# GpSimd's low parts of weights in four operations of 256 columns, and in the MLPs only behind the first two blocks

## The chip, the cores and the metric

The kernel runs on one core of a Trainium2 chip. The metric is the device time of one execution in microseconds (us).

## The reference, cut to what matters

A trunk of two layers for 256 tokens of width 1024 in f32. Layer 0 mixes tokens by native sparse attention (16 heads of 64), layer 1 by differential attention (8 heads, two softmax maps each). Every mixer is followed by an MLP of width 4096 with a squared ReLU. Each sub-layer has an RMS norm in front, with shift, scale and gate computed from a vector c (adaLN).

```python
for i in range(DEPTH):
    mod = cond @ w_ada[i] + b_ada[i]
    sh1, sc1, g1, sh2, sc2, g2 = jnp.split(mod, 6, axis=-1)
    h = rms_norm(x, ln_mix_g[i]) * (1.0 + sc1[:, None, :]) + sh1[:, None, :]
    ...
    x = x + g1[:, None, :] * y
    h = rms_norm(x, ln_mlp_g[i]) * (1.0 + sc2[:, None, :]) + sh2[:, None, :]
    x = x + g2[:, None, :] * (jnp.square(jax.nn.relu(h @ w_mlp_in[i])) @ w_mlp_out[i])
```

## The kernel before, in words

**Products in three parts.** Every f32 product of the large layers is made of three products of rounded numbers. A matrix w is split into a high part wh (w rounded to the type float32r) and a low part wl = w - wh, an activation h into hh and hl, and `mm3` (lines 79 to 83) adds wh*hh, wl*hh and wh*hl in PSUM: in the profile these are the matmuls of L81, L82 and L83. So each weight costs a load (L158, issued from SP's queue into a buffer wr), a high part (L202, a cast on ScalarE) and a low part (L206, a subtraction on VectorE or on GpSimd). VectorE is DVE in the profile, GpSimd POOL, ScalarE ACT and TensorE PE.

**Units and their order.** The weights are planned in a list of units of kind "w" of 128 x 1024 numbers (512 KB); the order in which they are planned is the order in which they are loaded and split. There are 32 units up to the end of the first mixer, 64 in an MLP (blocks of 512 columns: four units "up" and four units "dn" each), and 32 in the second mixer. Units of kind "a" and "p" between them are weights of the adaLN: "a" is multiplied by c and summed by VectorE (L227 and L232, 128 x 1024 each). `use(u)` (line 241) hands a unit's parts to its matmuls and first carries the list on to `look[0]` units from u, that is four units beyond u in the MLPs, where `look[0]` is 6; `issue` (line 152) keeps the loads ahead by `ahead_dma[0]`. All of wr, wh, wl and other tiles of this size share 32 buffers, so a load waits until one comes free.

**Which engine makes a low part.** `halves[0]` is a list of pairs (engine of the high part, engine of the low part). `do_unit` counts the "w" units and takes the entry that the count, modulo the list's length, points to:

```python
            pos["split"] += 1
            hi, lo = halves[0][pos["split"] % len(halves[0])]
```

In the mixers the list has two entries, the first with GpSimd (lines 1307 and 1328). `sublayer_end` (line 1167) sets it to VectorE alone for the end of a sub-layer and also makes the first four units of the next one. `mlp` (line 1196) sets it to three entries, the first with GpSimd (line 1294), then calls `up_first(2)` for the first two blocks, whose products are made for one half of the tokens and then the other, and then goes through the blocks with `up` and `down`. High and low parts stand under `tc.high_priority(-50)`: the framework plans each engine's order of instructions when the kernel is built, by its own estimate of their times, and these get a lower priority than what stands around them. On an engine, instructions then run in that fixed order.

**What stands around the lows.** `prenorm` (line 1143) makes the rows of a sub-layer's input: L570 on GpSimd (a power), L572 and L574 (scaling), transposes on TensorE (L1151), L1156 and L1159 (shift and scale), then L1163 (hh) and L1164 (hl) on VectorE, which the matmuls L81 to L83 of the MLP wait for. In the mixers VectorE normalises heads: L805, L305 to L311, L811 and L814 (which reads PSUM), the rotary steps L781, L784 and L785, whose result TensorE transposes (L793). In the first mixer it scales softmax rows (L1043, transposed at L1048); in the second it subtracts the two maps (L1365 to L1367, L1369, transposed at L1375), with L1391 on GpSimd and L1402 behind. L77 makes the low part of activations, L1014 the masked scores, and L920 on GpSimd prepares the compressed blocks (16 operations of 120 columns).

Of the kernel before, what the change touches and what calls it, by code (L numbers as in the profile page):

```python
# [19 lines left out]
F32 = mybir.dt.float32  # L20
# [3 lines left out]
ALU = mybir.AluOpType  # L24
# [18 lines left out]
def body(ctx: ExitStack, tc: tile.TileContext, a):  # L43
    nc = tc.nc
    vec, act, pool, pe = nc.vector, nc.scalar, nc.gpsimd, nc.tensor
# [9 lines left out]
    def bank(tag="tr"):  # L55
        return pp.tile([P, 512], F32, name=tag, tag=tag, bufs={"acc": 4, "sc": 2, "tr": 2}[tag])
# [4 lines left out]
    def w4(name, dt=F32):  # L61

        return wp.tile([P, 1024], dt, name=name, tag="w", bufs=32)
# [4 lines left out]
    def z4():  # L68
        return w4("z4", F32R).rearrange("p (i s) -> p i s", i=4)
# [4 lines left out]
    def split(h, l, src):  # L74

        act.copy(h, src)  # L76
        vec.tensor_tensor(l, src, h.bitcast(F32), op=ALU.subtract)  # L77

    def mm3(out, x, w, start, stop):

        pe.matmul(out, x[0], w[0], start=start, stop=False, skip_group_check=True)  # L81
        pe.matmul(out, x[0], w[1], start=False, stop=False, skip_group_check=True)  # L82
        pe.matmul(out, x[1], w[0], start=False, stop=stop, skip_group_check=True)  # L83
# [7 lines left out]
    halves = [[(act.copy, vec)]]  # L91
# [60 lines left out]
    def issue(n):  # L152
        while pos["dma"] < min(len(items), n):
            i = pos["dma"]
            pos["dma"] += 1
            raws[i] = w4("wr")
            for f, src in items[i]:
                nc.sync.dma_start(f(raws[i]), src)  # L158
# [7 lines left out]
    def ada_pe(rs, n, fin, hold, tag="tr"):  # L166
        m = n // P
        ps = bank(tag)
        for k in range(KT):
            c = k % 4  # L170
            w = rs[k * m // KT].rearrange("p (k n) -> p k n", n=n)[:, k % (KT // m)]
            pe.matmul(ps[32 * c : 32 * c + 32, 0:n], condz[:, k], w, start=k < 4, stop=k >= 4,  # L172
                      skip_group_check=True, tile_position=(0, 32 * c))
        acc = tmp()[:, 0:n]
        act.copy(acc, ps[:, 0:n])
        if hold is None:
            fin(acc)
        else:
            hold.append(lambda: fin(acc, ps[:, n:]))
# [3 lines left out]
    def flush(everything=True):  # L183

        for e in pend:
            e[0] -= 1
        while pend and (everything or pend[0][0] <= 0):
            pend.pop(0)[1]()

    def do_unit(u, hold=None):  # L190
        kind, i = units[u][0:2]
        if kind == "w":
            flush(False)
        issue(i + ahead_dma[0])
        r = raws.pop(i)
        if kind == "w":
            n = units[u][2]
            pos["split"] += 1
            hi, lo = halves[0][pos["split"] % len(halves[0])]
            h, l = (w4(x, F32R)[:, 0:n] for x in ("wh", "wl"))  # L200
            with tc.high_priority(-50):
                hi(h, r[:, 0:n])  # L202

            def low():
                with tc.high_priority(-50):
                    lo.tensor_tensor(l, r[:, 0:n], h.bitcast(F32), op=ALU.subtract)  # L206

            if hold is None:
                low()
            else:  # L210
                hold.append(low)
            done[u] = (h, l)
        elif kind == "p":
            n = units[u][3]
            rs = [r] + [raws.pop(i + j) for j in range(1, n // P)]
            if units[u][4]:
                late.append((rs, n, units[u][2]))
            else:
                ada_pe(rs, n, units[u][2], hold)
        else:  # L220
            _, _, st, k, fin, with_pool = units[u]
            with tc.high_priority(-50):
                if k == 0:
                    st["acc"] = w4("acc")
                c = cond[:, k : k + 1]
                if k == 0:
                    vec.tensor_scalar(st["acc"], r, c, None, op0=ALU.mult)  # L227
                elif with_pool:
                    vec.tensor_scalar(r, r, c, None, op0=ALU.mult)
                    pool.tensor_tensor(st["acc"], st["acc"], r, op=ALU.add)  # L230
                else:
                    vec.scalar_tensor_tensor(st["acc"], r, c, st["acc"], op0=ALU.mult, op1=ALU.add)  # L232
            if k == KT - 1:
                fin(st["acc"])
# [6 lines left out]
    def use(u, only=False):  # L241

        ahead = look[0] if only else 0
        for v in range(u, len(units)):
            if units[v][0] == "w":
                ahead += 1
                if v > u and ahead > look[0] - 1:
                    break
            done_to(v)
            if only:  # L250
                break
        h, l = done.pop(u)
        return lambda c, w: (h[:, c : c + w], l[:, c : c + w])
# [386 lines left out]
    for c0, src in ((0, a["nsa_q_gain"][:, 0:16]), (16, a["nsa_k_gain"][0, 1:2, 0:16]), (32, a["nsa_k_gain"][0, 2:3, 0:16]),  # L640
                    (48, a["diff_q_gain"][:, 0:16]), (64, a["diff_k_gain"][:, 0:16]), (80, a["nsa_b_gate"])):
        n = src.shape[1]
# [553 lines left out]
    def mlp(l):  # L1196
# [4 lines left out]
        def relu2(bk):  # L1201
            r = tmp()
            act.activation(r, bk, AF.Relu)  # L1203
            s2 = tmp()
            act.activation(s2, r, AF.Square)
            return s2

        def up_first(nb):

            zs = [(z4(), z4()) for _ in range(nb)]  # L1210
            hid.update(enumerate(zs))
            ws = {}

            def products(b, t):
                ts = slice(t * P, (t + 1) * P)
                if t == 0:
                    ws[b] = [[use(u) for u in U["up", l, b, f2]] for f2 in range(2)]
                bk = bank("sc")
                for f2 in range(2):
                    for k in range(KT):  # L1220
                        mm3(bk[:, f2 * 256 : f2 * 256 + 256], (hh[:, k, ts], hl[:, k, ts]),
                            ws[b][f2][k // 4](k % 4 * 256, 256), k == 0 and f2 == 0, k == KT - 1)
                return relu2(bk)

            def back(b, t, s2):
                ts = slice(t * P, (t + 1) * P)
                tb = bank()
                for j in range(4):
                    pe.transpose(tb[:, j * P : (j + 1) * P], s2[:, j * P : (j + 1) * P], ident)
                split(zs[b][0][:, :, ts], zs[b][1][:, :, ts], tb.rearrange("p (j s) -> p j s", j=4))  # L1230

            prev = None
            for t in range(2):
                for b in range(nb):
                    s2 = products(b, t)
                    if prev is not None:
                        back(*prev)
                    prev = (b, t, s2)
            back(*prev)
# [51 lines left out]
                    yield t, 2  # L1291

        look[0], ahead_dma[0] = 6, 14
        halves[0] = [(act.copy, pool), (act.copy, vec), (act.copy, vec)]
        nb = 2
        up_first(nb)
        while held:
            held.pop(0)()
        for b in range(1, NB):
            if b >= nb:  # L1300
# [20 lines left out]
                pairs(1, qT1, left.pop()), drain_last()), first)  # L1321
    sublayer_end(second, bks, (0, 0), 0, 1, U["up", 0, 0, 0] + U["up", 0, 0, 1], held)
    acc, last = mlp(0)
    sublayer_end(last, acc, (0, 1), 1, 0, U["dk", 0], held)

# [119 lines left out]
    weave(chain(after(*last), heads("F2 V3 S7 E7 C6 T6 . F3 V4 C7 T7 . F4 V5 . V6 F5 V7 F6 F7")), first)  # L1445
    sublayer_end(second, bks, (1, 0), 1, 1, U["up", 1, 0, 0] + U["up", 1, 0, 1], held)
    acc, last = mlp(1)
    ov = a["out"].rearrange("o (t p) d -> p (o t) d", p=P)
    flush()
# [55 lines left out]
```

## Time and profile before

| | |
|---|---|
| median of three runs | 722.15 us (720.5 to 722.8) |
| the profiled execution's own time | 721.25 us |
| its span in the profile | 719.1 us |
| matmuls | 4263, busy 682.3 us |
| low parts on VectorE, L206 | 132, busy 188.5 us |
| low parts on GpSimd, L206 | 60, busy 157.5 us |
| high parts, L202 | 192, busy 191.9 us |
| adaLN sums on VectorE, L232 | 49, busy 72.4 us |

All times within an execution are counted from the start of the span. The profile gives for each engine the time in which it was busy; in the lists of instructions the number in brackets at a row's end is how long the engine had been idle before it, and what ended that. Times of matmuls overlap, as they are pipelined.

### The profile page before, as it was taken

The page shows a single profiled execution, that of the slowest core. Times are in us where ns is not written, and L with a number is a line of the kernel's source. Part 1 is how long each engine was busy: PE and PEld are TensorE (multiplying, and loading weights), DVE is VectorE, ACT ScalarE, POOL GpSimd, SP SyncE. Part 2 cuts the span into 40 slices and gives each one's busy share as a digit, 9 for nine tenths or more (in the row PEclk, how much of TensorE's full clock was granted, in tenths as well). Part 3 has the DMA queues.
Part 4 walks back from the last instruction along what each step waited for, and adds up shares of the span by engine and source line. Part 5 has one row for each costly group of instructions (what it writes and reads, how often), then busy time and mean ns, then how long its engine had stood idle before and what let it go on. Part 6 is the DMA issues. An engine that isn't in the chain of part 4 may idle for free.

```text
span 719.1 us, 11663 instructions
## 1 busy us (share of the span) xinstructions
PE 682.3 (95%) x4263; PEld 565.1 (79%) x4263; DVE 493.1 (69%) x911; ACT 400.5 (56%) x779; POOL 200.5 (28%) x138
## 2 busy tenths in 40 slices
PE   8999889999988999999999999899979999999997
PEld 7787654656687988999896777667769888998896
DVE  4457879777869598858885987776782874235753
ACT  6646438769565345634453765786566355543650
POOL 4105311002023243233231634223222143323430
PEclk9999999999999999999999999999999999999999
DMA  9999999522828889989799254243744787755001
GB/s 289 331 334 373 325 307 289 150 75 91 263 87 274 279 298 370 331 286 319 262 358 350 81 159 170 94 118 92 243 164 138 261 280 229 231 180 176 1 1 58
DMA packets 105421, 156.67 MB, mean 218 GB/s; under 512 B 6135, under 2 KB 60180, under 8 KB 105364
## 3 DMA queue, kind: packets, MB, share of 16 engines
q1 hardware_dynamic: 103952, 153.60, 65.9%
q0 software_dynamic: 1248, 2.20, 1.1%
q8 instruction: 33, 0.54, 0.3%
q14 instruction: 24, 0.20, 0.1%
q10 hardware_dynamic: 164, 0.14, 0.1%
HBM read 154.86 MB, written 1.06 MB: 217 GB/s over the span
## 4 chain that ended last, share of the span: by engine, by line
PE 59%; DVE 17%; issue 11%; DMA 4%; ACT 4%; POOL 2%; SPq 1%; DVEq 0%; POOLq 0%; ACTq 0%
PE acc L83 9%; PE acc L81 8%; PE acc L82 8%; PE sc L83 8%; PE sc L81 7%; PE sc L82 7%; DVE wl L206 5%; DMA wr<-in_nsa_w_in_dram 3%; DVE acc L232 2%; PE sc L1008 1%; PE tr L172 1%; ACT wh L202 1%; PE tr L1048 1%; SPq L158 1%; POOL wl L206 1%
## 5 line engine op out<-in xcount | busy, mean ns | idle before, releaser
L206 POOL TENSOR_TENSOR wl<-wr,wh 128x1024 fp32r<-128x1024 f32 x60 | 157.5, 2628 | 363.2 <-ACT wh L202 298.0
L206 DVE TENSOR_TENSOR wl<-wr,wh 128x1024 fp32r<-128x1024 f32 (+1 forms) x132 | 188.5, 1443 | 63.3 <-ACT wh L202 46.2
L202 ACT CAST wh<-wr 128x1024 fp32r<-128x1024 f32 x192 | 191.9, 1032 | 47.4 <-PE acc L82 10.0
L81 PE MATMUL acc<-wh,z 128*128 128x512 f32 (+1 forms) x320 | 127.5, 398 | 0.0
L83 PE MATMUL acc<-wh,z 128*128 128x512 f32 (+1 forms) x320 | 125.2, 392 | 1.1 <-DVE z L77 1.1
L82 PE MATMUL acc<-wl,z 128*128 128x512 f32 (+1 forms) x320 | 125.2, 391 | 0.0
L81 PE MATMUL sc<-hh,wh 128*128 128x256 f32 x384 | 109.0, 284 | 0.0
L83 PE MATMUL sc<-hh,wl 128*128 128x256 f32 x384 | 108.7, 283 | 0.0
L82 PE MATMUL sc<-hl,wh 128*128 128x256 f32 x384 | 108.7, 283 | 0.0
L1203 ACT ACTIVATE t<-sc 128x512 f32<-128x512 f32 x32 | 19.1, 598 | 109.6 <-PE sc L83 109.5
L81 PEld LDWEIGHTS sc<-hh,wh 128*128 128x128 f32 x384 | 73.6, 192 | 1.3 <-issue 0.8
L82 PEld LDWEIGHTS sc<-hl,wh 128*128 128x128 f32 x384 | 73.7, 192 | 0.4
L232 DVE SCALAR_TENSOR_TENSOR acc<-wr,cond,acc 128x1024 f32<-128x1024 f32 x49 | 72.4, 1477 | 2.2 <-DMA wr<-in_w_ada_dram 1.5
L83 PEld LDWEIGHTS sc<-hh,wl 128*128 128x128 f32 x384 | 73.6, 192 | 0.0
L83 PEld LDWEIGHTS acc<-wh,z 128*128 128x128 f32 x320 | 60.1, 188 | 14.2 <-DVE z L77 2.0
L81 PEld LDWEIGHTS acc<-wh,z 128*128 128x128 f32 x320 | 60.2, 188 | 13.7 <-issue 1.9
L82 PEld LDWEIGHTS acc<-wl,z 128*128 128x128 f32 x320 | 60.2, 188 | 11.5 <-issue 0.6
L77 DVE TENSOR_TENSOR z<-t,z 128x512 fp32r<-128x512 f32 x24 | 26.7, 1113 | 60.3 <-ACT z L76 60.3
L82 PE MATMUL acc<-wl,hh 128*128 128x512 f32 (+1 forms) x160 | 61.1, 382 | 3.0 <-DVE wl L206 3.0
L81 PE MATMUL acc<-wh,hh 128*128 128x512 f32 (+1 forms) x160 | 63.1, 396 | 0.0
L83 PE MATMUL acc<-wh,hl 128*128 128x512 f32 (+1 forms) x160 | 60.5, 378 | 0.0
L83 PE MATMUL sc<-wh,hl 128*128 128x256 f32 (+1 forms) x152 | 44.1, 292 | 4.2 <-DVE hl L1164 4.1
(286 smaller groups left out, 1119.4 us busy)
## 6 DMA issues: line engine op xcount, KB each, us to landing
wr<-in_w_ada_dram SPq DMA_DIRECT2D x80, 512.0 KB, 5.9
wr<-in_w_mlp_in_dram SPq DMA_DIRECT2D x64, 512.0 KB, 4.9
wr<-in_w_mlp_out_dram SPq DMA_DIRECT2D x64, 512.0 KB, 4.4
wr<-in_diff_w_in_dram SPq DMA_DIRECT2D x24, 512.0 KB, 5.1
wr<-in_w_ada_dram SPq DMA_DIRECT2D x32, 256.0 KB, 6.8
wr<-in_nsa_w_in_dram SPq DMA_DIRECT2D x16, 512.0 KB, 7.3
wr<-in_nsa_w_out_dram SPq DMA_DIRECT2D x16, 256.0 KB, 10.4
wr<-in_diff_w_out_dram SPq DMA_DIRECT2D x8, 512.0 KB, 3.7
```

Source lines behind the costliest of these rows:

```text
L77: vec.tensor_tensor(l, src, h.bitcast(F32), op=ALU.subtract)
L81: pe.matmul(out, x[0], w[0], start=start, stop=False, skip_group_check=True)
L82: pe.matmul(out, x[0], w[1], start=False, stop=False, skip_group_check=True)
L83: pe.matmul(out, x[1], w[0], start=False, stop=stop, skip_group_check=True)
L158: nc.sync.dma_start(f(raws[i]), src)
L172: pe.matmul(ps[32 * c : 32 * c + 32, 0:n], condz[:, k], w, start=k < 4, stop=k >= 4, skip_group_check=True, tile_position=(0, 32 * c))
L202: hi(h, r[:, 0:n])
L206: lo.tensor_tensor(l, r[:, 0:n], h.bitcast(F32), op=ALU.subtract)
L232: vec.scalar_tensor_tensor(st["acc"], r, c, st["acc"], op0=ALU.mult, op1=ALU.add)
L1008: pe.matmul(p1, q[:, P:S], k, start=True, stop=True)
L1048: pe.transpose(tb[:, e * P : (e + 1) * P], s.pr[:, br, h, e * P : (e + 1) * P], ident)
L1203: act.activation(r, bk, AF.Relu)
```

## The change

The subtraction of a low part on GpSimd is written as operations of 256 columns (on VectorE it stays one), and in `mlp` the list with GpSimd is set after `up_first` and no longer before it, so that in `up_first` the list of `sublayer_end`, VectorE alone, holds.

```diff
             def low():
+                step = n if lo is vec else 256
                 with tc.high_priority(-50):
-                    lo.tensor_tensor(l, r[:, 0:n], h.bitcast(F32), op=ALU.subtract)
+                    for c in range(0, n, step):
+                        cs = slice(c, min(n, c + step))
+                        lo.tensor_tensor(l[:, cs], r[:, cs], h[:, cs].bitcast(F32), op=ALU.subtract)
...
         look[0], ahead_dma[0] = 6, 14
-        halves[0] = [(act.copy, pool), (act.copy, vec), (act.copy, vec)]
         nb = 2
         up_first(nb)
+        halves[0] = [(act.copy, pool), (act.copy, vec), (act.copy, vec)]
```

## Rows read from the trace of the kernel before

**Rows 1.** The page's first part: busy us, share of the span, instructions.

```profile
PE 682.3 (95%) x4263; PEld 565.1 (79%) x4263; DVE 493.1 (69%) x911; ACT 400.5 (56%) x779; POOL 200.5 (28%) x138
```

**Rows 2.** Busy time by stage: first MLP, second mixer, second MLP (the last columns clock, DMA).

```profile
205.00:385.00 180.00, 177.57 (x1164) 159.24 (x1165) 135.59 (x114) 87.63 (x114) 54.12 (x23) 1.00 0.86 295
405.00:515.00 110.00, 101.17 (x476) 78.19 (x475) 86.94 (x209) 73.72 (x183) 40.80 (x22) 1.00 0.42 130
535.00:705.00 170.00, 169.68 (x1100) 154.92 (x1099) 87.50 (x66) 84.45 (x107) 52.15 (x21) 0.99 0.50 158
```

**Rows 3.** TensorE's waits: who waited for whom, us in total, times, longest.

```profile
PE tr L793 <- DVE qn L785: 4.6, 5, 1.7
PE sc L83 <- DVE hl L1164: 4.1, 3, 1.8
...
PE tr L1229 <- DVE z L77: 1.6, 1, 1.6
...
PE tr L1375 <- DVE pr L1369: 1.5, 1, 1.5
```

**Rows 4.** Of tiles wl and hl: duration in ns, least, median, most; first and last start.

```profile
L206 POOL TENSOR_TENSOR wl<-wr,wh x60: 2369/2416/3482, 74.2 to 696.4; 128x1024 fp32r<-128x1024 f32 x60
...
L1164 DVE TENSOR_TENSOR hl<-t,hh x12: 684/693/2533, 197.7 to 536.0; 128x512 fp32r<-128x512 f32 x12
```

**Rows 5.** Timelines around 202 (start, us; engine by engine), and the matmul behind.

```profile
200.94 1.04 ACT L202 CAST wh<-wr 128x1024 fp32r<-128x1024 f32 x1
...
202.11 2.38 POOL L206 TENSOR_TENSOR wl<-wr,wh 128x1024 fp32r<-128x1024 f32 x1 [1.83 <-ACT wh L202]
...
202.51 2.53 DVE L1164 TENSOR_TENSOR hl<-t,hh 128x512 fp32r<-128x512 f32 x1
...
205.09 0.39 PE L83 MATMUL sc<-wh,hl 128*128 128x256 f32 x1 [1.79 <-DVE hl L1164]
...
207.71 1.22 DVE L206 TENSOR_TENSOR wl<-wr,wh 128x1024 fp32r<-128x1024 f32 x1
```

**Rows 6.** Timelines of POOL and of DVE from 406 to 414.

```profile
406.61 2.89 POOL L206 TENSOR_TENSOR wl<-wr,wh 128x1024 fp32r<-128x1024 f32 x1 [5.28 <-PE acc L83]
...
409.46 3.36 POOL L206 TENSOR_TENSOR wl<-wr,wh 128x1024 fp32r<-128x1024 f32 x1
...
407.74 2.83 DVE L206 TENSOR_TENSOR wl<-wr,wh 128x1024 fp32r<-128x1024 f32 x1
...
410.50 3.40 DVE L206 TENSOR_TENSOR wl<-wr,wh 128x1024 fp32r<-128x1024 f32 x1
```

**Rows 7.** Timelines near 71 (POOL, then DVE beside it), and L308 without GpSimd.

```profile
70.22 2.15 POOL L920 TENSOR_TENSOR z<-t,cols 128x120 f32<-128x120 f32 x5
...
71.52 0.48 DVE L308 TENSOR_TENSOR hnt<-hnr 128x16 f32<-128x16 f32 x1
...
415.83 0.17 DVE L308 TENSOR_TENSOR hnt<-hnr 128x16 f32<-128x16 f32 x1 [0.53 <-ACT hnr L307]
```

**Rows 8.** Timelines of POOL and DVE from 429 to 434.

```profile
429.75 2.40 POOL L206 TENSOR_TENSOR wl<-wr,wh 128x1024 fp32r<-128x1024 f32 x1 [7.93 <-ACT wh L202]
...
430.99 1.45 DVE L781 TENSOR_TENSOR ropeA<-qn,csg 128x256 f32<-128x256 f32 x1
432.36 0.41 DVE L781 TENSOR_TENSOR ropeB<-qn,csg 128x256 f32<-128x256 f32 x1
...
433.02 0.28 DVE L785 TENSOR_TENSOR qn<-ropeA,ropeB 128x128 f32<-128x128 f32 x1
```

**Rows 9.** Timelines of POOL and DVE from 473 to 476.

```profile
473.40 2.48 POOL L206 TENSOR_TENSOR wl<-wr,wh 128x1024 fp32r<-128x1024 f32 x1 [4.82 <-DVE dmn L1014]
...
473.56 2.59 DVE L1369 SCALAR_TENSOR_TENSOR pr<-pr,dcf 128x256 f32<-128x256 f32 x1
```

**Rows 10.** Busy time in a stretch late in the first MLP (columns as in rows 2).

```profile
318.00:340.00 22.00, 22.00 (x143) 20.11 (x143) 18.70 (x15) 9.15 (x12) 8.17 (x3) 1.00 0.92 329
```

**Rows 11.** Waits of SP's DMA queue.

```profile
SPq L158 <- POOL wl L206: 63.3, 17, 5.9
```

## The prediction

> **What bounds the kernel now.** I read the page's busy times first: TensorE is busy 95% of the span, VectorE 69%, ScalarE 56%, GpSimd 28% [rows 1]. By stage, TensorE is idle only 2.4 us of 180 in the first MLP and 0.3 of 170 in the second, while the 110 us of the second mixer leave 8.8 [rows 2]. So time can come only from TensorE's gaps in the mixers and at the entries of the MLPs. The waits of TensorE say who ends these: VectorE, through L785, L1164, L77, L1369 and others [rows 3]. Then I asked what makes VectorE late there. L1164 takes 0.69 us in the median and up to 2.53; a low part on GpSimd takes 2.37 to 3.48 [rows 4]. The long ones lie beside each other: at 202.11 a low starts on GpSimd, at 202.51 L1164 starts and ends 0.55 us after that low, and TensorE stands 1.79 us until 205.09 for it [rows 5]; the entry of the second MLP, at 531, repeats it. Two neighbouring lows show both directions. VectorE's wl, 1.22 us when nothing hinders it [rows 5], comes at 407.74 and ends 1.07 us after the first low is over (409.50); the second low is longer than 2.37 by 0.99; and VectorE's next wl takes 3.40 [rows 6]. So such an operation of VectorE (inputs in SBUF) and one of GpSimd exclude each other for a whole operation.
>
> **The change, part by part.**
>
> Quarters. Five pieces of L920, 120 columns each on GpSimd, take 2.15 us with small VectorE operations between, 0.43 from start to start [rows 7]. A low of 1024 columns takes 2.37 [rows 4], so a column costs (2.37-0.43)/904 = 2.15 ns and 256 columns 0.43+136x2.15 ns = 0.72 us: a low holds GpSimd 2.87 us instead of 2.37. Bounds: 0.59 (a quarter of 2.37) and 1.02 (0.43 on top of it). I take 0.72, since L920 is the same operation at half the size. [...]
>
> What VectorE then meets. An operation that comes while a quarter runs waits at most 0.72 us and not up to 2.4. But the next quarter waits behind it and goes before VectorE's next: L308, 0.17 us at 415.83, takes 0.48 beside L920, having waited for one piece [rows 7], and the second low above went before VectorE's second wl [rows 6]. So one long operation gains by the split, and a chain of short ones pays for all four pieces.
>
> Entries of the MLPs. up_first takes the units 4 to 11 of an MLP (its eight and the look-ahead of four, less the four made before). With 32 units before the first MLP and 128 before the second, GpSimd's turn falls on 6, 9, 12 and so on; 6 and 9 of each MLP move to VectorE, and 60 lows become 56, or 224 operations. With unit 6's low gone, L1164 takes 0.69 and the two gaps of 1.79 go: 3.58 us. The 1.22 us on VectorE are covered if they come behind L1164: unit 7, used after unit 6, is made at 207.71 only [rows 5], and no wait on it is in the view of the waits. Ahead of L1164 the cover is gone, and an entry keeps 0.57 of its 1.79. I take them behind: lows have the lower priority, and the cast ends at 201.98, only 0.53 us before L1164 starts [rows 5]. Unit 9 of the first MLP ran beside L227, in VectorE's queue ahead of the L77 that TensorE then waits 1.6 us for [rows 3]; on VectorE it costs 1.22 in the same queue. I take nothing, between 1.2 gained (2.4 held before, less 1.22) and 1.2 lost. In the second MLP VectorE is free there.
>
> Mixers. Nine gaps of TensorE end with a chain that a low delays. Two as patterns. At 429.75 a low starts; L781 comes at 430.99 and takes 1.45, and L785 ends at 433.30 [rows 8]. With quarters, two are over by 431.19, L781 (0.41) at 431.60, the third at 432.32, the second L781 at 432.72, the fourth at 433.44, L784 and L785 at 433.92: 0.6 us later. At 473.56 L1369's larger half waits out nearly a whole low and ends at 476.15 [rows 9]; with quarters the first is over by 474.12 and L1369 soon after 474.6: that gap of 1.5 [rows 3] goes. The same walk at the other seven gives +0.4 (gap until 81.6), +0.5 (179.6), +1.1 (423.7), -0.7 (452.8, two neighbouring lows), -0.6 (463.2), -0.7 (489.9, with L1366 and both L1369) and +0.5 (510.0). The nine sum to 1.4 us gained. Bounds: if VectorE's next operation goes first each time, the chains pay once and gain some 8.4; with quarters of 1.02 us the short chains lose, in all some -5.
>
> Late first MLP. From 318 to 340 VectorE is busy 18.7 of 22 us, with the DMA engines at 0.92, and TensorE has no gap [rows 10]; the stretch from 349 to 376 is as dense. Eighteen lows hold the port 0.5 us longer, five or six of them in these two, so a start 1.8 us earlier may not be kept: I subtract 1.0, between 0 and 3.2 (all of that, 3.0, and a little for the two lows moved). In the second MLP VectorE is busy 87.5 of 170 us [rows 2], which covers it: nothing.
>
> Loads and queues. SP's load queue waits 63 us in all for GpSimd lows to free their buffers [rows 11]; a low that yields to VectorE between its quarters ends later and delays such a load by as much. No wait of TensorE goes back to a load, so I take nothing; its cover gone, it would be part of the 3.2. Behind a low in GpSimd's own queue stand only L570 and L1391, in places where the low is already over or, at L1391, as part of the walk above.
>
> Sum: 3.6+0+1.4-1.0 = 4.0 us. The profiled execution took 721.25 (span 719.1 and 2.15 around it), which makes 717.25; the median shown, 722.15, is 0.9 above it, so I predict 718.2.
>
> **The rivals.**
> 1. VectorE goes first whenever both wait. For it: the second L781 and L785 of rows 8 follow what stands before them at once, so VectorE's next operation is ready when one ends. Against it: [rows 6, 7], where GpSimd gets the port between two of them. Mixers +8.4, so 3.6+8.4-1.0 = 11.0: 711.2.
> 2. The moved low comes ahead of L1164. For it: its cast is over before L1164 starts [rows 5]. Against: the priority. 2x0.57+1.4-1.0 = 1.5 us: 720.6, no change that can be told.
> 3. The port isn't given up between quarters. Against it stands the turn that VectorE got between two lows [rows 6]; for it, that these were two whole lows with separate casts. The price: ten lows in the nine chains hold 0.5 us more each, 5 us lost and 1.4 not gained; 3.6-5.0-1.0 = -2.4, so 724.6, slower. It decides once a VectorE wl that meets a low still lasts over 3 us. [...]
> 4. The late first MLP takes all of it, VectorE and DMA being near full there: 3.2 instead of 1.0, and the mixers at 0.7 as with quarters of 0.75: 3.6+0.7-3.2 = 1.1, so 721.1, no change.
>
> **How the numbers follow.** A measurement of this kernel tells some 0.3%, 2.2 us, from no change. Forecast 0.50 (its own range 715.5 to 720.4), rival 1 0.10, rival 2 0.13, rival 3 0.10, rival 4 0.11, and 0.06 for quarters near 1.02 (about 724). Faster: 0.47 of the forecast's 0.50 and rival 1, 0.57. Same: the rest of it, rivals 2 and 4, 0.27. Slower: rival 3 and the long quarters, 0.16. The range leaves out most of rival 1 and half of the slow cases: 713.4 to 723.2.
>
> **What would show it.** Right: 224 lows on GpSimd of about 0.7 us; L1164's longest near 0.7 and no gap of 1.79 before L83; VectorE's wl mostly under 2 us; L781, L784 and L785 each longer in the norms and their gaps no shorter; the gap before L1375 near 476 gone. Wrong: wl still near 3.4 (rival 3); a wl between the cast and L1164 (rival 2); new gaps of TensorE between 320 and 376 (rival 4); L781 to L785 in a row while a low stands half done (rival 1).

## The result, and the profile after

The kernel with the change takes 710.3 us in the median against 721.3 us of the kernel before (four executions; the 722.15 of the table in front was of three): 0.9838 of its time (95% interval 0.981 to 0.9866), 11 us faster. The prediction was 718.2, with a range of 713.4 to 723.2: the direction was right, and the gain is almost three times the 4.0 us forecast. The profiled execution took 710.62 us, with a span of 708.8.

The page's first part answers [rows 1] (busy us, share of the span, instructions):

```profile
PE 678.1 (96%) x4263; PEld 561.6 (79%) x4263; DVE 464.1 (65%) x915; ACT 399.5 (56%) x779; POOL 271.0 (38%) x302
```

VectorE (DVE) spends 29 us less, though it has four more lows to make, and GpSimd (POOL) 71 us more: what VectorE no longer waits for the port, GpSimd now spends on more operations and on waits between them. (The port is what the prediction calls the thing at which an operation of VectorE with its inputs in SBUF and one of GpSimd exclude each other, as in [rows 5] and [rows 6].) The stages answer [rows 2]: first MLP, second mixer, second MLP, the windows shifted by what the kernel is ahead.

```profile
203.00:382.00 179.00, 178.58 (x1175) 160.17 (x1174) 129.19 (x118) 88.45 (x118) 89.23 (x76) 1.00 0.86 298
402.00:507.00 105.00, 100.33 (x475) 78.11 (x473) 79.03 (x207) 73.81 (x183) 54.06 (x64) 1.00 0.42 134
525.00:695.00 170.00, 169.24 (x1106) 154.46 (x1107) 79.18 (x70) 85.12 (x110) 75.72 (x74) 1.00 0.50 161
```

In the second mixer TensorE's idle time fell from 8.8 us to 4.7; the MLPs stay full. The tile rows (duration in ns: least, median, most) answer [rows 4], and two waits of TensorE answer [rows 3]:

```profile
L209 POOL TENSOR_TENSOR wl<-wr,wh x224: 721/746/1802, 77.0 to 689.7; 128x256 fp32r<-128x256 f32 x112
...
L1167 DVE TENSOR_TENSOR hl<-t,hh x12: 684/689/693, 198.7 to 527.5; 128x512 fp32r<-128x512 f32 x12
```

```profile
PE tr L796 <- DVE qn L788: 4.2, 3, 3.1
...
PE acc L83 <- DVE z L77: 1.2, 2, 0.8
```

The quarters last 0.72 to 0.75 us where nothing holds them up, as predicted. L1167 (L1164 before) never waits any more. What was L785's 4.6 us in five waits is now three, of which the one of 3.1 lies in the first mixer; the wait of L1375 at 476 and the 1.6 us for L77 in the first MLP are gone.

**Where the time went.** Taking the same matmul in both traces, the difference of its start shows by how much a kernel is ahead there. The table gives what each stretch adds (us, negative is gained; times are those of the kernel before). GpSimd makes no low before 74 us, and yet the profiled executions of the kernels below lie between 0.1 us ahead and 2.8 behind there; so the first column is mostly scatter, and the others are read stretch by stretch. A stretch can be read only where its matmuls keep their order: in the row of the mixers' lows on VectorE the matmul at 200.9 has another place, so that row goes by the one at 201.3.

```
                                 to     entry   L77    rest    second  entry   clock    540.5
                                200.9  MLP 1  to 236  MLP 1   mixer   MLP 2  to 540.5  to 560
the change                      +1.0    -1.9   -2.0    -0.0    -4.5    -1.8    -1.5    +0.4
the change, again               +1.2    -1.8   -2.0    -0.0    -4.5    -1.9    -1.5    +0.4
quarters alone                  -0.4    -1.6   -0.9    -0.1    -4.5    -1.6    -1.5    +0.4
move alone                      +3.0    -1.8   -1.4    -0.0    -0.0    -1.8    -1.5    +0.0
quarters in the mixers          +1.8    -0.0   +0.1    -0.0    -4.5    +0.0    -1.5    +0.0
quarters in the MLPs            +2.6    -1.6   -0.9    -0.0    -0.0    -1.6    -1.5    +0.4
halves                          +1.2    -1.9   -1.6    -0.0    -3.4    -1.9    -1.5    +0.2
eighths / again             -0.4/-2.1   -1.9   -2.4    -0.0  -0.1/-4.1 -1.9    -1.5    +1.0
two of three lows on GpSimd     -0.1    -1.5   -2.0    -0.0    +1.5    -1.8    -1.5    +0.4
mixers' lows on VectorE         +2.2    -1.5   -2.0    -0.0    -5.7    -1.9    -1.5    +0.4
second mixer's on VectorE       +1.3    -1.9   -2.0    -0.0    -5.9    -1.8    -1.5    +0.5
first lows on VectorE           -1.0    -1.3    -2.0    -0.0    -4.5    -1.8    -1.5    +0.4
VectorE's own in halves         -0.4    -1.8    -2.2    -0.0    -4.3    -2.2    -1.5    +0.5
the last two together           -1.2    -1.8    -2.2    +0.0    -4.3    -2.2    -1.5    +0.5
the best version                -0.2    -1.8   -2.2    +0.0    -7.6    -2.7    -1.4    +0.5
```

The column "clock" is no part of the gain. Behind the second MLP's entry the profiled execution of the kernel before had a granted clock of 0.72 on average, and its 256-column matmuls took 0.41 us for a time, not 0.28 (from 536 to 538, where the one below lies, the granted clock was 0.50). No other kernel's profile shows it there, not even that of quarters in the mixers alone, which has the same gap of 1.79 us in front; whether other executions of the kernel before have it, no trace shows. First the window of before and one of its matmuls, then the window of that kernel (columns as above):

```profile
534.00:540.00 6.00, 5.97 (x37) 5.97 (x38) 4.80 (x7) 3.15 (x6) 0.00 (x0) 0.72 0.01 3
```

```profile
536.25 0.41 PE L83 MATMUL sc<-wh,hl 128*128 128x256 f32 x1
```

```profile
531.40:537.40 6.00, 5.98 (x50) 5.98 (x51) 4.80 (x7) 4.27 (x7) 0.00 (x0) 1.00 0.01 3
```

### The profile page after: what moved, and what is told of

Read it like the earlier page. It is cut to its first block, busy times and chain, and to the rows that moved or that the text cites. A ratio compares the mean times of both kernels' runs of the same rounds, so it can differ in the third digit from the quotient of the medians.

```text
span 708.8 us, 11840 instructions
## 1 busy us (share of the span) xinstructions
PE 678.1 (96%) x4263; PEld 561.6 (79%) x4263; DVE 464.1 (65%) x915; ACT 399.5 (56%) x779; POOL 271.0 (38%) x302
## 5 line engine op out<-in xcount | busy, mean ns | idle before, releaser
L209 POOL TENSOR_TENSOR wl<-wr,wh 128x256 fp32r<-128x256 f32 x224 | 228.2, 1050 | 292.6 <-ACT wh L202 243.8
L209 DVE TENSOR_TENSOR wl<-wr,wh 128x1024 fp32r<-128x1024 f32 (+1 forms) x136 | 176.5, 1311 | 77.1 <-ACT wh L202 65.7
L77 DVE TENSOR_TENSOR z<-t,z 128x512 fp32r<-128x512 f32 x24 | 20.1, 839 | 62.6 <-ACT z L76 62.6
L81 PE MATMUL sc<-wh,hh 128*128 128x256 f32 (+1 forms) x152 | 43.8, 289 | 2.1 <-DVE hh L1166 2.1
## 6 DMA issues: line engine op xcount, KB each, us to landing
wr<-in_nsa_w_out_dram SPq DMA_DIRECT2D x16, 256.0 KB, 10.6
```

Source lines behind the costliest of these rows:

```text
L209: lo.tensor_tensor(l[:, cs], r[:, cs], h[:, cs].bitcast(F32), op=ALU.subtract)
```

## The experiments

The theory that the table suggested: the quarters gave the second mixer its 4.5 us because taking turns at the port costs VectorE less than the prediction charged. The rival: turns cost what was charged, and the gain beyond the prediction is that of the moved lows and of the order that the plan makes of them.

### Each part alone

Quarters alone keep the old place of the list (the edit shown is against the kernel after); the move alone is the kernel before with the list moved, so it keeps whole lows:

```diff
-        nb = 2
-        up_first(nb)
         halves[0] = [(act.copy, pool), (act.copy, vec), (act.copy, vec)]
+        nb = 2
+        up_first(nb)
```

> Theory 1 (a handover between VectorE and GpSimd costs less than the full lengths of the two operations, so that short chains hardly pay for the quarters): the mixers keep the 4.4 us that they gained between 403 and 511; unit 6's low still stands beside L1164, but as quarters, so that each gap of 1.79 us shrinks to about 0.4 (2.8 us), the slower clock behind the second goes (1.4), and the L77 gap loses about 1.0: 9.6 us in all, near 711.7. Theory 2 (the chains pay as the prediction had it, and what came on top is the moved lows with the order of work that follows from them): 1.4 + 2.8 - 1.0 = 3.2 us, near 718.1.

Measured: 712.44 us, ratio 0.9866 (0.9841 to 0.9892).

> Theory 1: the mixers stay as before; the two entries give 3.7 us, the clock behind the second 1.4, the L77 gap 1.7 to 2.2: 6.8 to 7.3 us, near 714.3. Theory 2: all that came on top of the prediction is here: 3.7 + 1.4 + 2.2 and some of the 4.4 us of the mixers, 9 us or more, near 712. If the prediction's own terms hold (entries alone, late first MLP without quarters free): 3.6, near 717.7.

Measured: 715.48, ratio 0.9906 (0.9881 to 0.993). The mixers stay as before and the entries give 1.8 us each. Quarters in one place only, with the list in its old place (here the mixers, whose list has two entries; `== 2` makes it the MLPs):

```diff
-                step = n if lo is vec else 256
+                step = n if lo is vec or len(halves[0]) == 3 else 256
```

> Quarters only where the list has two entries (the two mixers), whole lows and the old list in the MLPs. Theory 1: 4.4 us, near 716.9, and both gaps of 1.79 us stay. Theory 2: 1.4 us, near 719.9.

Measured: 716.44, ratio 0.9921 (0.9897 to 0.9946).

> Quarters only where the list has three entries (the two MLPs), old list. Theory 1: 2.8 + 1.4 + 1.0 = 5.2 us, near 716.1, and this and the run with quarters in the mixers add up to the run with quarters alone. Theory 2: 2.8 - 1.0 = 1.8 us, near 719.5, with new gaps of TensorE between 318 and 376.

Measured: 716.26, ratio 0.9912 (0.9886 to 0.9937), with no gap over 0.4 us between 318 and 376.

All four are nearer to the first theory than to the rival; in these executions the kernel before took 723.2 in the median, so the ratios are the safer figures. The second mixer gains 4.5 us wherever it has quarters, and nothing where it has not. The entries are gained by either part: with quarters alone L1167 waits out the rest of one quarter (0.90 us instead of 2.53), and the gap of 1.79 shrinks to 0.16 (VectorE and GpSimd, then the matmul behind):

```profile
201.72 2.77 POOL L209 TENSOR_TENSOR wl<-wr,wh 128x256 fp32r<-128x256 f32 x3 [1.83 <-ACT wh L202]
...
202.13 0.90 DVE L1167 TENSOR_TENSOR hl<-t,hh 128x512 fp32r<-128x512 f32 x1
```

```profile
203.08 0.39 PE L83 MATMUL sc<-wh,hl 128*128 128x256 f32 x1 [0.16 <-DVE hl L1167]
```

So the parts overlap there: by the table the move adds only 1.5 us to the quarters (0.2 at each entry, 1.1 at L77).

### What a turn costs

A kernel of phases, each a chain of one size on VectorE beside one size on GpSimd.

> This kernel leaves out all of the computation: it runs chains of subtractions on VectorE (each reads what the one before wrote, both inputs in SBUF unless said) beside a series of them on GpSimd, in phases, ten of each, and each also alone. Alone, from the traces: VectorE 0.41 us for 256 columns, 0.20 for 128, 1.21 for 1024; GpSimd 0.72 for 256, 2.37 for 1024. Theory 1 (a handover costs less than both lengths): a pair of 256 columns on each engine recurs every 0.88 to 0.90 us, with GpSimd at 1024 columns every 2.6, and VectorE at 1024 with GpSimd at 256 every 1.7; by turns, one to one. Theory 2 (one waits out the whole of the other): 1.13, 2.78 and 1.93 us. With one of VectorE's inputs in PSUM, both theories expect no exclusion: 0.41 and 0.72 as alone.

Measured, as groups of the timeline (start, length of the whole group, xcount): VectorE alone with 256 columns, then beside GpSimd's 128, 256, 512 and 1024; VectorE's 1024 beside 256; and with one input in PSUM beside 256:

```profile
13.79 3.64 DVE L44 TENSOR_TENSOR dv<-dv,di 128x256 f32<-128x256 f32 x8 [0.71 <-ACT pi L40]
...
76.57 5.76 DVE L44 TENSOR_TENSOR dv<-dv,di 128x256 f32<-128x256 f32 x10 [44.08 <-ACT pi L40]
83.30 8.19 DVE L44 TENSOR_TENSOR dv<-dv,di 128x256 f32<-128x256 f32 x10 [0.96 <-ACT pi L40]
92.72 13.21 DVE L44 TENSOR_TENSOR dv<-dv,di 128x256 f32<-128x256 f32 x10 [1.23 <-ACT pi L40]
107.70 22.73 DVE L44 TENSOR_TENSOR dv<-dv,di 128x256 f32<-128x256 f32 x10 [1.77 <-ACT pi L40]
...
142.00 16.19 DVE L44 TENSOR_TENSOR dv<-dv,di 128x1024 f32<-128x1024 f32 x10 [1.30 <-ACT pi L40]
...
193.00 7.24 DVE L44 TENSOR_TENSOR dv<-dv,ps 128x256 f32<-128x256 f32 x16 [2.85 <-ACT pi L40]
```

Alone, an operation starts every 0.46 us (3.64 / 8). Beside quarters it is every 0.86 us ((8.19 - 0.46) / 9), one to one, where 0.42 and 0.72 end to end would be 1.14. Beside 128 columns it is 0.59, beside 512 1.42, beside 1024 2.47; VectorE's 1024 beside quarters 1.66. So at every turn the pair takes about 0.3 us less than its two lengths together. With an input in PSUM there are no turns: 0.45 us (7.24 / 16), as alone (3.60 / 8), and GpSimd's eight quarters beside it take 6.35 us, alone 6.32. So these subtractions exclude each other where both of VectorE's inputs are in SBUF, as the prediction read it from [rows 5] and [rows 6], and not with one in PSUM; but not for a whole operation, as it had it: a pair is over those 0.3 us sooner.

### Other piece sizes

```diff
-                step = n if lo is vec else 256
+                step = n if lo is vec else 512
```

> The kernel after, with two operations of 512 columns in place of four of 256 (each about 1.3 us alone). Theory 1: a single VectorE operation waits up to 1.1 us and not 0.5, a chain of four that meets two neighbouring lows pays 4 x 1.1 and not 4 x 0.5: the second mixer gives 1.5 to 3 us of its 4.6, the total is 712 to 713.5. Theory 2 (each handover costs full lengths, so that many pieces hurt chains): halves are at least as good as quarters, 710.5 or less.

Measured: 712.6, ratio 0.9867 (0.9836 to 0.9898), 1.1 us lost in the second mixer: somewhat under the first theory's 1.5 to 3, against the rival. With 128 in place of 512:

> The kernel after, with eight operations of 128 columns (about 0.43 us each, 3.4 us a low). Theory 1: a VectorE operation that meets one waits 0.2 to 0.3 us and not 0.5, a chain of four gains 1 us more: some five such chains lie in front of gaps, 2 to 4 us, so 706.5 to 708.5; the longer lows cost nothing in the MLPs. Theory 2: the chains meet eight handovers and not four, and the lows last 0.5 us longer beside the dense stretches of the first MLP: no gain, 710 to 713.

Measured: 712.38, ratio 0.9856 (0.9821 to 0.9891): the first theory missed, and the rival's 710 to 713 holds it. The profile, of the slowest of the six executions (715.19), shows one wait that nobody expected. L784, ready at 411.78, ends 6.46 us later, and in that time 15 pieces of GpSimd end, one behind the other; it ends 0.29 us after the last piece of the two lows, at 417.95, so VectorE went only when GpSimd had none left. TensorE then stands 2.62 us (VectorE, GpSimd, TensorE):

```profile
411.78 6.46 DVE L784 TENSOR_TENSOR ropeA<-qn,csg 128x256 f32<-128x256 f32 x1
418.16 0.41 DVE L784 TENSOR_TENSOR ropeB<-qn,csg 128x256 f32<-128x256 f32 x1
```

```profile
411.19 6.76 POOL L209 TENSOR_TENSOR wl<-wr,wh 128x128 fp32r<-128x128 f32 x16
```

```profile
420.17 1.11 PE L796 MATMUL tr<-first,qn 128*128 128x128 f32 x4 [2.62 <-DVE qn L788]
```

The same kernel once more:

> The same kernel as the one with eighths. If the wait of 6.46 us at the L784 near 412 belongs to the order of the instructions, it is there again; if it hangs on the moment at which VectorE arrives, it is gone or elsewhere, and the gap near 420 is under 1.5 us and not 2.6.

Measured, in a single execution: 707.95. The same L784 takes 0.58 us there, and its gap is under 0.3:

```profile
410.08 0.58 DVE L784 TENSOR_TENSOR ropeA<-qn,csg 128x256 f32<-128x256 f32 x1
410.58 0.68 DVE L784 TENSOR_TENSOR ropeB<-qn,csg 128x256 f32<-128x256 f32 x1
```

So the long wait hangs on the moment, not on the order. Even without it the second mixer gains 4.1 us, not more than with quarters, so the 2 to 4 us that were expected of eighths aren't there. One reason is in this trace: the small L1394 of GpSimd (L1391 in the kernel before) starts only at 499.15, behind six pieces in GpSimd's own queue, though what it reads was there at 497.12; VectorE's L1397 waits 2.36 us for it, and TensorE 1.56 us, until 500.54. In the kernel after TensorE waits 1.02 us at this place, in the kernel before 0.15. To find the moment, VectorE was made to arrive at many points of a piece:

> This kernel leaves out all of the computation: beside series of GpSimd subtractions that do not depend on each other (96 of 128 columns, 64 of 256, 40 of 512) VectorE does 24 subtractions of 256 columns (in a fourth phase of 128, beside 128), each behind a copy out of PSUM that is 16 columns longer each time, so that they arrive at many points of a piece. Theory 1a (the turn is given by the pieces: a waiting VectorE operation always goes before the next piece): the longest wait is one piece, so VectorE's 256 columns take at most 0.42 + 0.45 us beside 128, 0.42 + 0.75 beside 256 and 0.42 + 1.3 beside 512. Theory 1b (GpSimd's next piece, already issued, can go first, as in the run with eighths, where one L784 took 6.46 us while 15 pieces ended): with pieces of 128 some of the 24 wait for two or many pieces, with 256 few and with 512 none.

Measured: no operation waits for more than one piece. The longest of 24 beside 128, 256 and 512 columns (ns: least, median, most):

```profile
L51 DVE TENSOR_TENSOR dv<-dv,di x24: 407/430/645, 12.8 to 30.0; 128x256 f32<-128x256 f32 x24
```

```profile
L51 DVE TENSOR_TENSOR dv<-dv,di x24: 407/582/806, 59.6 to 79.3; 128x256 f32<-128x256 f32 x24
```

```profile
L51 DVE TENSOR_TENSOR dv<-dv,di x24: 426/1140/1345, 109.8 to 141.3; 128x256 f32<-128x256 f32 x24
```

What lets GpSimd go 15 times in the kernel stays open.

### Fewer and more lows on GpSimd

```diff
-    halves[0] = [(act.copy, pool), (act.copy, vec)]
+    halves[0] = [(act.copy, pool), (act.copy, pool), (act.copy, vec)]
```

> The kernel after, with two of three lows of the mixers on GpSimd and not one of two. VectorE loses some seven lows of 1.21 us; GpSimd gets 28 more quarters, each of which holds up one VectorE operation by about 0.4 us (0.86 a pair against 0.46) if it meets one. Theory 1: 28 x 0.4 = 11 us at most against 8.5 us, so between 2 us faster and 2 slower, 708 to 712. Theory 2: 28 x 0.72 = 20 us against 8.5, slower by some us: 713 or more.

Measured: 713.71, ratio 0.9866 (0.9842 to 0.989): out of the first theory's range and in the rival's (713 or more), with 6 us less gained in the second mixer. The first theory's estimate counted every low that leaves VectorE as if it stood in front of a gap; that this is why it missed was not tried. The other way round, with `[(act.copy, vec)]` in both mixers:

> The kernel after, with every low of the two mixers on VectorE, so that no turns are taken there: 20 lows of 1.21 us (24 us) come to VectorE, and some 80 quarters go, which by the isolated pairs cost VectorE 0.4 us each where they meet an operation with both inputs in SBUF. From the trace of the kernel after, VectorE's operations are lengthened by 46 us in all, some 15 of it in the second mixer. Theory 1: 24 us more for some 25 less, but a whole low of 1.21 stands in VectorE's queue ahead of the chains: 1 to 5 us slower than the change, 711 to 715. If the turns were what is left to gain: faster, 706 to 709.

Measured: 710.0, ratio 0.9838 (0.9816 to 0.9861), between the two ranges expected. The second mixer gains 1.2 us more; the first loses some 1.6 from 73.5 to 201.3 us. So in the second alone:

> The kernel after, with the lows of the second mixer alone all on VectorE. Theory 1 (what the quarters gave there is waiting for the port, and the rest of that waiting is still worth more than the 14 lows of 1.21 us that come to VectorE): 1.0 to 1.5 us below the change, 709 to 709.6, and the stretch from 400 to 523 us gains 5.7 against the kernel before, not 4.4. If the first mixer's order had changed what reaches the second: no gain, 710.5.

Measured: 709.14, ratio 0.9831 (0.9806 to 0.9856), and 5.9 us gained in that stretch. So there even quarters cost more than the 14 lows weigh on VectorE: what the change gained in it is waiting that it took away, and 1.4 us of it is left. Half of that is no wait for the port: with the change 0.8 us are lost at the L1394 that stands behind quarters in GpSimd's own queue (510.0, below); here TensorE waits at most 0.2 us there.

### Towards a better version

With the first weave's lows on VectorE (the list with GpSimd is set behind it):

```diff
-    halves[0] = [(act.copy, pool), (act.copy, vec)]
     cg = compress()
...
     weave(chain(kv_post(), take(cg, 7)), g0)
+    halves[0] = [(act.copy, pool), (act.copy, vec)]
```

> The kernel after, with the lows of the first mixer's first weave (to the end of kv_post) on VectorE alone. The gap of 3.1 us that ends at L796 near 84 stands behind four L784 of 0.82 us that alternate with GpSimd's quarters, and alone take 0.2. Theory 1: these four give back 2.2 us, and the two or three lows that come to VectorE cost 1.2 each where they stand ahead of L787: between 2 us gained and 1 lost, 708.5 to 711.5. If instead the gap is set by the load or the matmuls of the projection, nothing changes: 710.5.

Measured: 709.95, ratio 0.9827 (0.9796 to 0.9858). The gap at 84 goes (3.0 us), and 2.5 us of it are given back by 120. Without that edit, but with VectorE's own lows cut as well:

```diff
-                step = n if lo is vec else 256
+                step = 512 if lo is vec else 256
```

> The kernel after, with VectorE's own lows also cut, into two of 512 columns (about 0.68 us each), so that the plan can put a short operation between them. If the gaps that are left in the mixers (1.3 to 3.1 us) end with chains behind a whole low of 1.22 us on VectorE: 1 to 2 us gained, near 709. If they don't: 136 lows cost 0.1 to 0.15 us more each, which is covered outside the mixers: 710 to 711.

Measured: 708.61, ratio 0.9798 (0.9777 to 0.9818). Behind 200.9 us the table shows only 0.2 us more than for the change, so where the rest comes from is not shown. Both together, and the change again beside them:

> The kernel after, with VectorE's own lows in two of 512 columns and the first weave's lows of the first mixer on VectorE alone. If both gains are real and lie in different stretches (the first before 85 us, the second from 404 to 424): 1 to 2 us below the change itself. If the first is given back by 120 us, as its trace suggests: the same as with VectorE's halves alone, about 1 us below.

Measured: 708.19, ratio 0.9821 (0.9797 to 0.9844).

> The kernel after, again, beside the two variants that came out near or ahead of it: 0.981 to 0.987 of the time before, as measured first.

Measured: 710.57, ratio 0.9847 (0.9822 to 0.9871). Last, both together with the second mixer's lows on VectorE:

> The same with VectorE's own lows in two operations of 512 columns, and the first weave's lows of the first mixer on VectorE: both changes of the best variant so far. If the gains add: 708.2 less 1.0 to 1.5, near 707. If VectorE's halves gained in the second mixer by what they let through between GpSimd's turns, that part falls away: near 708.2.

Measured: 705.73, ratio 0.9788 (0.9765 to 0.9811), some 4 to 5 us below the change (0.9847, 0.9822 to 0.9871), and faster than both kernels; 4 us of it lie in the stretches behind 200.9. The second mixer gains 7.6 us there: halves of VectorE's lows help where VectorE makes them all (5.9 with whole ones).

## Why the prediction was wrong

**The mixers' term (1.4 us) was mis-sized; it measured some 6.** The step that failed is the walk of "Mixers. Nine gaps of TensorE end with a chain that a low delays", which charged both operations' lengths at each turn and left out waits of single operations. That VectorE and GpSimd alternate one to one was right, and rival 1, whose 711.2 lies nearest the result, is not what happened: VectorE didn't go first. But a turn of 256 columns costs VectorE 0.40 us more than alone (0.86 - 0.46) and not 0.72. [Rows 6] had it: a low of 2.37 and a wl of 1.22 make 3.59, and the wl took 3.40. By the price measured, a chain of four pays about a whole us less than it was charged. Gap by gap in the second mixer, predicted and measured gains: at 423.7 1.1 and 1.6; at 433.45 -0.6 and 0; at 452.8 (with the small gap at 448.7 in front of it) -0.7 and 1.55; at 463.2 -0.6 and -0.35; at 476.2 1.5 and 1.6; at 489.9 -0.7 and 0.15; at 510.0 0.5 and -0.1: together 0.5 and 4.5. The single wait of [rows 9] came out as walked; the chains did not: at 423.7, 433.45, 452.8, 463.2 and 489.9 together they gave 4.4 us more than walked, of which 1.0 has another cause (437.3, below). That the other 3.4 are all cheaper turns is argued from their sign and size; the one at 452.8 was followed. Before (VectorE, then GpSimd):

```profile
444.04 1.45 DVE L781 TENSOR_TENSOR ropeA<-qn,csg 128x256 f32<-128x256 f32 x1
445.41 2.62 DVE L781 TENSOR_TENSOR ropeB<-qn,csg 128x256 f32<-128x256 f32 x1
448.07 0.29 DVE L784 TENSOR_TENSOR qn<-ropeA,ropeB 128x128 f32<-128x128 f32 x1
448.28 0.28 DVE L785 TENSOR_TENSOR qn<-ropeA,ropeB 128x128 f32<-128x128 f32 x1
```

```profile
442.79 4.96 POOL L206 TENSOR_TENSOR wl<-wr,wh 128x1024 fp32r<-128x1024 f32 x2 [3.99 <-ACT wh L202]
```

After:

```profile
438.62 0.48 DVE L784 TENSOR_TENSOR ropeA<-qn,csg 128x256 f32<-128x256 f32 x1
439.02 0.96 DVE L784 TENSOR_TENSOR ropeB<-qn,csg 128x256 f32<-128x256 f32 x1
440.01 0.71 DVE L787 TENSOR_TENSOR qn<-ropeA,ropeB 128x128 f32<-128x128 f32 x1
440.65 0.82 DVE L788 TENSOR_TENSOR qn<-ropeA,ropeB 128x128 f32<-128x128 f32 x1
441.40 3.44 DVE L209 TENSOR_TENSOR wl<-wr,wh 128x1024 fp32r<-128x1024 f32 x2
```

Two whole lows held the chain from 444.04 to 448.56, 4.52 us; four quarters hold it 2.85. The two wl behind it take 3.44 instead of 2.35 (they meet quarters too), which gives back 1.1 of the 1.7. From L781 to the end of the two wl that is 0.6 gained, where the full lengths, walked from the same start, give 0.7 lost. The other 1.0 at this gap came before the chain, at a wl of VectorE that met a whole low and was not in the walk; before, then after:

```profile
437.30 2.58 DVE L206 TENSOR_TENSOR wl<-wr,wh 128x1024 fp32r<-128x1024 f32 x1 [2.86 <-ACT wh L202]
```

```profile
432.85 1.61 DVE L209 TENSOR_TENSOR wl<-wr,wh 128x1024 fp32r<-128x1024 f32 x1 [2.86 <-ACT wh L202]
```

The gap at 510.0 closes (0.7 gained), and 0.8 is lost right behind it, where the prediction took the lows in GpSimd's own queue to be over, or counted in the walk: L1394 (L1391 before) stands there behind quarters, VectorE waits for it, and TensorE for VectorE (kernel after):

```profile
503.10 0.61 DVE L1397 TENSOR_SCALAR qn<-tr,dnr 128x128 f32<-128x128 f32 x2 [1.66 <-POOL dnr L1394]
```

```profile
503.77 0.44 PE L1402 MATMUL tr<-first,qn 128*128 128x128 f32 x2 [1.02 <-DVE qn L1397]
```

In the first mixer 0.9 was predicted, at the gaps until 81.6 and 179.6. The first can't be told: five of the seven profiles from before to quarters in the MLPs have a slower granted clock in parts of 73 to 90 us (0.67 to 0.81 in their slowest stretch of 4 or 5 us). From 95 to 200.9 us the kernel with the change gained 1.6 us in both its profiles, quarters alone and quarters in the mixers 1.0 each, and the two kernels with whole lows nothing. Of this 0.5 came at 171.8 to 179.6, as predicted, and the rest at the gap of 1.31 us at 100.5, which was not among the nine. It stands behind a single operation that waited out a low; before, then after:

```profile
97.24 1.97 DVE L310 TENSOR_SCALAR crt<-crt 128x32 f32<-128x32 f32 x1
```

```profile
99.87 0.32 DVE L313 TENSOR_SCALAR crt<-crt 128x32 f32<-128x32 f32 x1
```

**Unit 9 ("I take nothing") measured 2.0 us.** The bounds of 1.2 either way counted L227's wait and the low that comes to VectorE. The step left out the plan: with the low in VectorE's queue it also puts one of the sums of L232 (1.28 us) behind the L77 that TensorE waits for. Before and after, VectorE's own order:

```profile
216.86 2.52 DVE L227 TENSOR_SCALAR acc<-wr,cond 128x1024 f32<-128x1024 f32 x1 [6.61 <-PE sc L83]
219.41 2.60 DVE L232 SCALAR_TENSOR_TENSOR acc<-wr,cond,acc 128x1024 f32<-128x1024 f32 x2
...
223.07 2.60 DVE L232 SCALAR_TENSOR_TENSOR acc<-wr,cond,acc 128x1024 f32<-128x1024 f32 x2
...
226.72 1.28 DVE L77 TENSOR_TENSOR z<-tr,z 128x512 fp32r<-128x512 f32 x2
```

```profile
215.57 1.23 DVE L209 TENSOR_TENSOR wl<-wr,wh 128x1024 fp32r<-128x1024 f32 x1 [5.55 <-ACT wh L202]
216.71 0.75 DVE L230 TENSOR_SCALAR acc<-wr,cond 128x1024 f32<-128x1024 f32 x1
217.49 1.28 DVE L235 SCALAR_TENSOR_TENSOR acc<-wr,cond,acc 128x1024 f32<-128x1024 f32 x1
...
219.83 2.60 DVE L235 SCALAR_TENSOR_TENSOR acc<-wr,cond,acc 128x1024 f32<-128x1024 f32 x2
...
223.48 1.28 DVE L77 TENSOR_TENSOR z<-tr,z 128x512 fp32r<-128x512 f32 x2
```

Four sums stand ahead of L77 before, three after. L227 takes 1.77 us less and one sum of 1.28 is gone from the queue; the low that came starts in idle time, at 215.57, and delays L227 (L230 after) by only 0.66 against the matmuls: it starts at 216.71, where 216.86 less the 0.81 that the kernel is ahead would be 216.05. So L77 starts 2.4 us earlier, and the gap of 1.57 closes whole: 1.7 were measured there and 0.3 at the gap at 232.1 behind it. Without the sum L77 would be 1.1 us earlier, within the bounds. With quarters alone, where nothing is reordered, the first gap gave 0.4.

**The entries (3.58) were right:** 1.9 and 1.8. The moved low came behind L1167, as taken (rival 2 fell).

**The late first MLP (-1.0) didn't come:** 0.02 to 0.04 us from 236 to 398 in every kernel, with quarters or without; nothing of the start was lost (rival 4 fell). Rival 4's 0.7 for the mixers rests on no run: the quarters took the 0.75 that it assumed, 0.746 in the median, and the mixers gave some 6. The second MLP, put at nothing, lost 0.4 at 549, with quarters only. Rival 3 (the port isn't given up) doesn't occur with quarters: in the kernel after no wl of VectorE takes over 1.78 us, where before the longest took 3.43. Something like it did once with eighths (the L784 of 6.46 us).

The sum by what was measured: 1.6 + 1.9 + 2.0 + 0.0 + 4.5 + 1.8 - 0.4 = 11.4 us, against 11.0 and 10.6 between the medians of the two measurements. The first term is read behind 95 us alone.

## What to carry to other kernels

Where two engines exclude each other, take the price of a turn from a pair in the trace (both lengths less what the pair took) before walking a chain with it: an error of 0.3 us a turn, some four turns a chain, was up to 3.4 of the 7 us missed here. Look as well for single operations that wait out a whole low, and for what stands behind the pieces in the other engine's own queue: the first were about 2 us that the walk left out, the second took 0.8 back. A low-priority operation that another engine must wait out belongs in pieces of the length of the operations that wait (here 256 columns: the second mixer gained 4.5 us, with 512 3.4, with 128 0.1 and 4.1), and in a stage of short chains it may be best on the waiting engine itself (5.9 there). When an edit moves work into a queue that a planner orders, ask what else the planner will move.

## What was not expected of the hardware

With pieces of 128 columns GpSimd once went 15 times running while one L784 of VectorE took 6.46 us. In a repetition the same L784 took 0.58, in the kernel after, with quarters, none took over 0.99, and the longest of 96 isolated arrivals took 1.35, beside 512 columns. In the chains of pairs the engines went one to one (every 0.59 us beside 128 columns). Here 14 pieces that started after 411.78 went ahead of the L784 that the profile has waiting since then, which turns of one to one don't explain.
